# Output projection regrouped into passes of six and two heads, a later square sum for retention heads, one Newton square on ScalarE, and the norm weights stored behind x's first rows

## The chip, the core and the metric

The kernel runs on one core of a Trainium2 chip. The core has a matrix engine (PE), a vector engine (DVE), a scalar engine (ACT), a general engine (POOL) and a queue engine (SP) that issues most transfers. Each engine works through its own program in order and waits on semaphores for the others. The metric is device time in microseconds (us) of one execution; lower is better. Times before: 1225.84 us, the median of three runs (1225.83 to 1226.55). Matrix products are accumulated in PSUM, of which there are eight banks of 128 x 512 float32.

## What is computed

Two layers over 512 tokens of width 1024, float32. Cut to what matters here:

```python
for l in range(DEPTH):
    h = rms_norm(x, norm1_g[l])
    rq, rk, rv, rg, sq, sk, sv = jnp.split(h @ w_in[l], IN_SPLITS, axis=-1)
    ret = chunk_retention(rotary(rq), rotary(rk), rv)          # 4 heads of 128
    ret = head_group_norm(ret, ret_norm_g[l]) * jax.nn.silu(rg)
    sb = head_rms_norm(stick_breaking(sq, sk, sv), sb_norm_g[l])  # 4 heads of 128
    x = x + jnp.concatenate([ret, sb], axis=-1) @ w_out[l]
    h = rms_norm(x, norm2_g[l])
    x = x + (jax.nn.silu(h @ w_gate[l]) * (h @ w_up[l])) @ w_down[l]
return rms_norm(x, final_g)
```

## The kernel before

All activations lie transposed, features on the 128 partitions and the 512 tokens along the row: `x` is eight tiles of 128 x 512, one for each 128 features. Every float32 matrix is split into a high and a low part (`hi` rounded by ACT, `lo = src - hi` by DVE or POOL), and one product of 128 x 128 by 128 x 512 is three matrix instructions (`mm3`, L188). The weights come as 205 units of 128 x 1024 (`WeightStream`, L98): SP loads a unit into `wraw`, ACT rounds it into `whi` (L130), DVE takes `wlo` (L131). There are three `whi`/`wlo` buffers, so the conversion of a unit can start when PE is through with the unit three before it. 24 matrix instructions use up one unit.

PE's order is written out by hand. `Stream` (L149) counts the planned time of what has been emitted, and `pe.later(delay, fn)` puts a piece of work into the stream once that much planned time has passed. The orders of the other engines are made by a scheduler at build time and are fixed in the program.

In the attention half of a layer PE computes, head by head, the projections of four stick-breaking heads (keys 4 to 7 of `mix`) and then of four retention heads (keys 0 to 3). A retention head h goes through these steps:

- `rotated` (L430): its q and its k come off the `acc` banks by DVE (L433 to L435, results `t1` and `t2`), POOL adds the two (L437), ACT rounds the sum (`qhi`, `khi`, L288), POOL takes the rest (`qlo`, `klo`, L289).
- `retain` (L561), D_RQK = 9000 ns after its k: PE forms the scores in `z` banks (the *score products*), DVE multiplies them with the decay (`p`, four instructions, L578), ACT and DVE split them (`pthi`, `ptlo`).
- `mixed` (L583), D_RAV = 9000 ns later: PE multiplies the scores with v into the bank `o`, 12 instructions. They are called the *weighted products* W0 to W3 below, for heads 0 to 3. DVE reads `o` into `m` (L587), and `normed` (L480) has ACT square `o` (L483), ACT and POOL split the square (`shi`, `slo`).
- `finish` (L488), D_SS = 5500 ns later: PE sums the squares over the features with two products by ones, again into the bank `o`. They are called the *square sum* SS0 to SS3. Then ACT takes Ln and Exp (L313, L314), and DVE refines the result by one Newton step (L315, L318, L321) and multiplies `m` (L494); ACT and DVE split `m` into `mix[h]`.

There is one bank with the tag `o`. W0, SS0, W1, SS1, W2, SS2, W3, SS3 follow each other in it: SS h can be written when L587 and L483 have read W h, and W h+1 can be written when Ln (L313) and the Newton instruction that reads the sum (L318) are done with SS h.

The output projection (L628 to L642) makes 8 x 8 products. First a pass over all eight output tiles d with the four stick-breaking heads, added to `x` (L632). Then, in two groups of four tiles, a pass with retention heads 0 to 2 for each tile, a drain of what is still due in the stream, and the products of head 3, added to `x` (L641); `feed` (L297) then prepares the tile for the FFN. The products of the first pass lie among the steps of the last retention heads and cover their chains.

At the start ACT issues the transfer of the norm weights `gcol` (128 x 48, L242), SP those of `x` and the first weight units. PE runs 12 warm-up products (`WARM`) without use. The first conversions follow in the order `hhi[0]` from x and `gcol` (L291), a square for the norm (L301), `whi` of the first unit in two halves.

Of the kernel before, what the change touches and what calls it, by code (L numbers as in the profile page):

```python
# [38 lines left out]
BY_KEY = ((0,), (1, 3), (2,))  # L39
WARM = 12  # L40
RAW = 4
D_SQK, D_TURN, D_STEP, D_SAV = 5000, 11500, 2000, 5000
D_RQK, D_RAV, D_SS = 9000, 9000, 5500

# [4 lines left out]
def block_plan():  # L49
# [6 lines left out]
    for l in range(L):  # L56
# [5 lines left out]
        for h in range(NH):  # L62
            plan += cols("w_in", l, RQ + h * HD) + cols("w_in", l, RK + h * HD)
        for d in range(KT):
            plan += [("w_out", l, NH + k, d * P, P) for k in range(NH)]
        for d0 in range(0, KT, 4):
            ds = range(d0, d0 + 4)
            plan += [("w_out", l, k, d * P, P) for d in ds for k in range(NH - 1)]
            plan += [("w_out", l, NH - 1, d * P, P) for d in ds]
        for k in range(KT):  # L70
# [27 lines left out]
class WeightStream:  # L98
# [11 lines left out]

    def load(self, upto, step=UW):
        for i in range(len(self.raw), min(upto, len(self.units))):
            w = sum(b[4] for b in self.units[i])
            raw = self.rawpool.tile([P, UW], F32, tag="wraw", name=f"wraw{i}", bufs=RAW)
            for a in range(0, w, step):
                c = slice(a, min(a + step, w))
                load = self.nc.sync.dma_start(out=raw[:, c], in_=self.ws[i, :, c])
            self.raw.append((raw, w))
            self.loads.append(load.ins)

    def split(self, upto, step=UW):
        nc = self.nc
        self.load(upto)
        for i in range(len(self.ready), min(upto, len(self.units))):
            raw, w = self.raw[i]
            hi = self.pool.tile([P, UW], F32R, tag="whi", name=f"whi{i}", bufs=3)
            lo = self.pool.tile([P, UW], F32R, tag="wlo", name=f"wlo{i}", bufs=3)
            for a in range(0, w, step):
                c = slice(a, min(a + step, w))
                copy = nc.scalar.copy(out=hi[:, c], in_=raw[:, c])  # L130
                nc.vector.tensor_tensor(  # L131
                    out=lo[:, c], in0=raw[:, c], in1=hi[:, c].bitcast(F32), op=ALU.subtract
                )
# [15 lines left out]
class Stream:  # L149
# [20 lines left out]
    def run(self, i):  # L170
        self.inside = True
        self.tasks.pop(i)[1]()
        self.inside = False

    def drain(self):
        while self.tasks:
            self.run(min(range(len(self.tasks)), key=lambda n: self.tasks[n][0]))

# [26 lines left out]
@with_exitstack  # L205
def layers(ctx, tc, xT_in, ws_in, gcol_in, gfin_in, cos_in, sin_in, dec_in, out):
    nc = tc.nc
# [32 lines left out]

    gcol = const.tile([P, L * NG], F32, name="gcol")
    nc.scalar.dma_start(out=gcol, in_=gcol_in)  # L242
    table_set(EXP_LN)
    idle = const.tile([P, S], BF16, name="idle")
    nc.vector.memset(idle, 0.0)
    x = [keep.tile([P, S], F32, name=f"x{k}", tag=f"x{k}") for k in range(KT)]
    for k in range(KT):
        nc.sync.dma_start(out=x[k], in_=xT_in[:, k, :])
        if k == 0:
            wst.load(1, step=512)  # L250
        elif k % 2 == 0:
            wst.load(1 + k // 2)
# [29 lines left out]
    def banks_b():  # L282
        return [bank() for _ in range(3)] + [bank("o", 1)]
# [60 lines left out]
    def attention(l):  # L344
        g0 = l * NG
        with tc.tile_pool(name=f"at{l}", bufs=1, reuse_waits="tile") as sb:
# [4 lines left out]
            def temp(name, bufs=4):  # L351
                return sb.tile([P, S], F32, tag="tmp", name=name, bufs=bufs)
# [127 lines left out]
            def normed(o, m, key):  # L480
# [147 lines left out]
            for d in range(KT):  # L628
# [4 lines left out]
            for d0 in range(0, KT, 4):  # L633
# [188 lines left out]
```

## Time and profile before

| | |
|---|---|
| runs, median | 1225.84 us |
| the profiled execution | 1226.61 us |
| its span, first to last instruction | 1224.8 us |
| PE busy | 1210.2 us, 99% of the span |
| DVE busy | 692.4 us, 57% |
| ACT busy | 489.4 us, 40% |
| POOL busy | 154.0 us, 13% |
| chain that ended last | PE 94%, DVE 4%, ACT 1%, DMA 1% |

The profile is read here in four steps. The page tells which engine fills the span. The list of waits of PE tells what it waits for. The timelines of the engines around such a wait tell which instruction in which queue was late. The view of stretches gives the granted PE clock, at 1.00 for 2.4 GHz and at 0.50 for 1.2 GHz. The profile models the end of a product 0.16 us after the next one can start, so a wait that it lists is about that much shorter than what PE loses. Layer 1 repeats layer 0 about 602.9 us later.

### The profile page before, as it was taken

What the parts mean: (1) busy time and instruction counts of PE and PEld (TensorE: products, weight loads), DVE (VectorE), ACT (ScalarE), POOL (GpSimd) and SP (SyncE); (2) the same over time, 40 slices, a digit from 0 to 9 for tenths busy, and PEclk for the clock granted to TensorE, in tenths of its full rate; (3) what the DMA queues carried; (4) which work ended last, traced back from release to release, by engine and by line L of the source; (5) the groups of instructions that cost most, each with busy time, mean ns of one, the idle gap of its engine ahead of it and who ended that gap; (6) DMA issues with size and microseconds to landing.
All of it is one profiled execution on the core that took longest, in us unless ns stands there. A gap on an engine that the chain in (4) does not pass through costs nothing.

```text
span 1224.8 us, 13905 instructions
## 1 busy us (share of the span) xinstructions
PE 1210.2 (99%) x5476; PEld 998.5 (82%) x5476; DVE 692.4 (57%) x868; ACT 489.4 (40%) x708; POOL 154.0 (13%) x135
## 2 busy tenths in 40 slices
PE   9999999999999999999999999999999999999997
PEld 6888887888888888888888888878888888888886
DVE  6566899774443344444444778997644433444433
ACT  6467644453331222323335755445432312223323
POOL 1122054120000000000121212523100000000021
PEclk9999999999999999999999999999999999999999
DMA  7321221223222222233232122213222223332311
GB/s 258 104 69 69 87 87 69 69 103 104 88 102 102 88 103 93 97 104 107 100 109 80 70 80 75 86 69 103 104 86 89 101 80 105 108 102 88 103 69 69
DMA packets 33329, 115.74 MB, mean 94 GB/s; under 512 B 3824, under 2 KB 3824, under 8 KB 33264
## 3 DMA queue, kind: packets, MB, share of 16 engines
q1 hardware_dynamic: 33120, 114.83, 27.1%
q8 instruction: 43, 0.70, 0.2%
q14 instruction: 22, 0.18, 0.0%
q10 hardware_dynamic: 144, 0.02, 0.0%
HBM read 112.75 MB, written 2.10 MB: 94 GB/s over the span
## 4 chain that ended last, share of the span: by engine, by line
PE 94%; DVE 4%; issue 1%; ACT 1%; DMA 1%; POOL 0%; SPq 0%; DVEq 0%; ACTq 0%
PE acc L185 73%; PE z L185 16%; PE o L185 5%; PE z L196 1%; DMA wraw<-ws 1%; DVE ptlo L289 1%; DVE wlo L131 1%; DVE u L315 0%; DVE mlo L289 0%; POOL slo L289 0%; DVE m L587 0%; DVE t L435 0%; DVE t L433 0%; DVE p L578 0%; DVE rn L321 0%
## 5 line engine op out<-in xcount | busy, mean ns | idle before, releaser
L130 ACT CAST whi<-wraw 128x1024 fp32r<-128x1024 f32 (+1 forms) x205 | 214.7, 1048 | 495.7 <-PE acc L185 225.1
L185 PE MATMUL acc<-hhi,whi 128*128 128x512 f32 x960 | 376.0, 392 | 0.0
L185 PE MATMUL acc<-hhi,wlo 128*128 128x512 f32 x960 | 373.9, 389 | 0.0
L185 PE MATMUL acc<-hlo,whi 128*128 128x512 f32 x960 | 373.8, 389 | 0.0
L131 DVE TENSOR_TENSOR wlo<-wraw,whi 128x1024 fp32r<-128x1024 f32 (+1 forms) x205 | 256.9, 1254 | 132.8 <-ACT whi L130 132.0
L185 PEld LDWEIGHTS acc<-hhi,wlo 128*128 128x128 f32 x960 | 180.2, 188 | 38.0
L185 PEld LDWEIGHTS acc<-hhi,whi 128*128 128x128 f32 x960 | 180.4, 188 | 36.3
L185 PEld LDWEIGHTS acc<-hlo,whi 128*128 128x128 f32 x960 | 180.4, 188 | 36.0
L691 DVE TENSOR_TENSOR u<-acc,rs 128x512 f32<-128x512 f32 x40 | 27.7, 692 | 134.4 <-PE acc L185 134.4
L305 POOL TENSOR_TENSOR ssq<-ssq,sqx 128x512 f32<-128x512 f32 x21 | 33.9, 1613 | 383.3 <-ACT sqx L304 382.8
L688 DVE TENSOR_TENSOR g<-acc,rs 128x512 f32<-128x512 f32 x40 | 27.7, 692 | 89.8 <-PE acc L185 89.8
L185 PE MATMUL acc<-ahi,whi 128*128 128x512 f32 x176 | 68.5, 389 | 0.0
L185 PE MATMUL acc<-alo,whi 128*128 128x512 f32 x176 | 68.5, 389 | 0.0
L185 PE MATMUL acc<-ahi,wlo 128*128 128x512 f32 x176 | 68.5, 389 | 0.0
L755 POOL TENSOR_TENSOR xtd<-xtd,gfin 128x512 f32<-128x512 f32 x7 | 10.2, 1453 | 345.7 <-ACT fsq L751 345.7
L292 DVE SCALAR_TENSOR_TENSOR hlo<-x,gcol,hhi 128x512 fp32r<-128x512 f32 x32 | 34.9, 1099 | 8.2 <-ACT hhi L291 8.2
L185 PEld LDWEIGHTS acc<-ahi,wlo 128*128 128x128 f32 x176 | 33.0, 188 | 6.9
L185 PEld LDWEIGHTS acc<-ahi,whi 128*128 128x128 f32 x176 | 33.0, 188 | 6.8
L185 PEld LDWEIGHTS acc<-alo,whi 128*128 128x128 f32 x176 | 33.0, 188 | 6.8
L288 ACT CAST ahi<-u 128x512 fp32r<-128x512 f32 x44 | 27.4, 622 | 28.1 <-DVE u L692 28.1
L185 PE MATMUL acc<-mhi,whi 128*128 128x512 f32 x88 | 35.8, 406 | 0.0
L185 PE MATMUL acc<-mhi,wlo 128*128 128x512 f32 x88 | 35.6, 405 | 0.0
(190 smaller groups left out, 1817.1 us busy)
## 6 DMA issues: line engine op xcount, KB each, us to landing
wraw<-ws SPq DMA_DIRECT2D x203, 512.0 KB, 3.5
x<-xT SPq DMA_DIRECT2D x8, 256.0 KB, 7.0
dec<-dec SPq DMA_DIRECT2D x8, 256.0 KB, 3.6
out<-ob SPq DMA_DIRECT2D x4, 512.0 KB, 2.6
wraw<-ws SPq DMA_DIRECT2D x2, 256.0 KB, 4.1
cosrs<-cos SPq DMA_DIRECT2D x2, 256.0 KB, 4.7
sinrs<-sin SPq DMA_DIRECT2D x2, 256.0 KB, 4.9
gfin<-gfin SPq DMA_DIRECT2D x1, 512.0 KB, 4.4
```

Of the source, the lines that this page charges most:

```text
L130: copy = nc.scalar.copy(out=hi[:, c], in_=raw[:, c])
L131: nc.vector.tensor_tensor(out=lo[:, c], in0=raw[:, c], in1=hi[:, c].bitcast(F32), op=ALU.subtract)
L185: self.nc.tensor.matmul(ps, lhsT=lhsT, rhs=rhs, start=start, stop=stop)
L196: self.nc.tensor.transpose(out, src, ident)
L288: nc.scalar.copy(out=hi, in_=src)
L289: eng.tensor_tensor(out=lo, in0=src, in1=hi.bitcast(F32), op=ALU.subtract)
L292: eng.scalar_tensor_tensor(out=lo, in0=src, scalar=scale, in1=hi.bitcast(F32), op0=ALU.mult, op1=ALU.subtract,)
L305: eng.tensor_tensor(out=ssq, in0=ssq, in1=q, op=ALU.add)
L688: nc.vector.tensor_tensor(out=g, in0=pg, in1=rs, op=ALU.mult)
L691: nc.vector.tensor_tensor(out=u, in0=pu, in1=rs, op=ALU.mult)
L755: nc.gpsimd.tensor_tensor(out=y, in0=y, in1=gfin[:, c], op=ALU.mult)
```

## The change

1. **Passes.** The eight output tiles are no longer gone through with the four stick-breaking heads first. A pass of six heads (`FIRST`: 4 to 7 and 0, `NEXT`: 1) goes over all tiles; in its first three tiles head 1 is held back until the other fifteen products are out. A pass of two heads (2 and 3) follows: over tiles 0 to 3 head 2, a drain, head 3; over tiles 4 to 7 both at once. The order of the weights in memory follows. The number of products and of additions to `x` is the same.
2. **Square sum later.** For retention heads the delay of `finish` is 9000 ns (`D_RSS`) in place of 5500.
3. **Newton.** In `normed` the first instruction of the Newton step (`-0.5/n * r * r`, L315 on DVE) becomes a Square on ACT, and the last two (L321, L494) are folded so that three DVE instructions are left of four. The results lie in two of the four `tmp` buffers.
4. **Start.** The norm weights lie behind the first 128 rows of x in one tile `xg` of 128 x 560, one transfer. x's second tile is issued between the two halves of the first weight unit. The first square is placed behind the rounding of the first half. `WARM` is 10.

```diff
-D_RQK, D_RAV, D_SS = 9000, 9000, 5500
+D_RQK, D_RAV, D_SS, D_RSS = 9000, 9000, 5500, 9000
+FIRST, NEXT = tuple(range(NH, 2 * NH)) + (0,), (1,)
+OUT = [((0, 1, 2), FIRST), ((0, 1, 2), NEXT), (range(3, KT), FIRST + NEXT)]
+OUT += [(range(4), (2,)), (range(4), (3,)), (range(4, KT), (2, 3))]
...
+            with tc.issue_after(wst.first_copy) if g == 0 else nullcontext():
+                nc.scalar.activation(out=ssq, in_=x[k], func=AF.Square)
...
-                    rn = temp("rn")
-                    rsqrt(rn, ss, HD)
-                    nc.vector.tensor_tensor(out=m, in0=m, in1=rn, op=ALU.mult)
+                    r, t = temp("rn"), temp("sq")
+                    nc.scalar.activation(out=r, in_=ss, func=AF.Ln, scale=1.0 / HD, bias=eps)
+                    nc.scalar.activation(out=r, in_=r, func=AF.Exp, scale=-0.5)
+                    nc.scalar.activation(out=t, in_=r, func=AF.Square, scale=0.125)
+                    nc.vector.scalar_tensor_tensor(
+                        out=t, in0=ss, scalar=HD * EPS, in1=t, op0=ALU.add, op1=ALU.mult
+                    )
+                    nc.vector.scalar_tensor_tensor(
+                        out=t, in0=t, scalar=6.0, in1=r, op0=ALU.subtract, op1=ALU.mult
+                    )
+                    nc.vector.scalar_tensor_tensor(
+                        out=m, in0=m, scalar=-0.25, in1=t, op0=ALU.mult, op1=ALU.mult
+                    )
...
-                pe.later(D_SS, finish)
+                pe.later(D_RSS if key < NH else D_SS, finish)
...
+                while k not in mix:
+                    pe.advance()
...
+    def advance(self):
+        self.run(min(range(len(self.tasks)), key=lambda n: self.tasks[n][0]))
...
+    xg = keep.tile([P, S + L * NG], F32, name="xg", tag="xg")
+    gcol = xg[:, S:]
...
+            wst.load(1, step=512, x1=lambda: nc.sync.dma_start(out=x[1], in_=xT_in[:, 0, :]))
...
+            def add(d, ps):
+                nc.vector.tensor_tensor(out=x[d], in0=x[d], in1=ps, op=ALU.add)
...
-            for d in range(KT):
-                ps = bank()
-                for k in range(NH):
-                    out_step(ps, d, NH + k, k == 0, k == NH - 1)
-                nc.vector.tensor_tensor(out=x[d], in0=x[d], in1=ps, op=ALU.add)
-            for d0 in range(0, KT, 4):
-                pss = dict(zip(range(d0, d0 + 4), banks_b() if d0 else banks_a()))
-                for d, ps in pss.items():
-                    for k in range(NH - 1):
-                        out_step(ps, d, k, k == 0, False)
-                pe.drain()
-                for d, ps in pss.items():
-                    out_step(ps, d, NH - 1, False, True)
-                    nc.vector.tensor_tensor(out=x[d], in0=x[d], in1=ps, op=ALU.add)
-                    feed(d, g0 + 8)
+            half = FIRST + NEXT
+            pss = [bank() for _ in range(3)]
+            for d, ps in enumerate(pss):
+                for k in FIRST:
+                    out_step(ps, d, k, k == half[0], False)
+            for d, ps in enumerate(pss):
+                for k in NEXT:
+                    out_step(ps, d, k, False, k == half[-1])
+                add(d, ps)
+            for d in range(3, KT):
+                ps = bank()
+                for k in half:
+                    out_step(ps, d, k, k == half[0], k == half[-1])
+                add(d, ps)
+            pss = banks_a()
+            for d, ps in enumerate(pss):
+                out_step(ps, d, 2, True, False)
+            pe.drain()
+            for d, ps in enumerate(pss):
+                out_step(ps, d, 3, False, True)
+                add(d, ps)
+                feed(d, g0 + 8)
+            for d in range(4, KT):
+                ps = bank()
+                out_step(ps, d, 2, True, False)
+                out_step(ps, d, 3, False, True)
+                add(d, ps)
+                feed(d, g0 + 8)
```

How this moves instructions is shown at two places of layer 0, as the built programs have them. Line numbers of the changed program are its own there: L193 is `mm` (L185 before), L133 and L135 are the rounding of a weight unit and its rest, L301 and L302 a split, L447 to L449 `rotated`, L497 the square of `o`, L507 to L516 the new `finish`, L611 is L587, L655 is `add`.

PE, place one, SS0 and what follows it in the program before (`acc` products are the projections of the last retention heads):

```order
L185 MATMUL acc<-hhi_130,wlo_1598 128x512
L185 MATMUL o<-shi,ones_r 128x512
L185 MATMUL o<-slo,ones_r 128x512
L185 MATMUL acc<-hhi_131,whi_1597 128x512
L185 MATMUL acc<-hlo_139,whi_1597 128x512
L185 MATMUL acc<-hhi_131,wlo_1598 128x512
```

The same place now, as far as the first product of W1:

```order
L193 MATMUL acc<-hhi_134,wlo_1590 128x512
L193 MATMUL o<-shi,ones_r 128x512
L193 MATMUL o<-slo,ones_r 128x512
L193 MATMUL acc<-hhi_127,whi_1631 128x512
L193 MATMUL acc<-hlo_135,whi_1631 128x512
L193 MATMUL acc<-hhi_127,wlo_1632 128x512
L193 MATMUL acc<-hhi_128,whi_1631 128x512
L193 MATMUL acc<-hlo_136,whi_1631 128x512
L193 MATMUL acc<-hhi_128,wlo_1632 128x512
L193 MATMUL o<-pthi,vhi 128x512
```

Before, 24 products lie between SS0 and W1 and 18 between the score products and SS0; now 6 lie between SS0 and W1 and 36 ahead of SS0. In the same way the products between SS1 and W2 go from 27 to 9, and those between SS2 and W3 from 33 to 12.

ACT, place one, from the rounding of a weight unit ahead of SS0's Ln (`r<-o`) to the square of W1, before:

```order
L130 CAST whi_1736<-wraw_1643 128x1024
L313 ACTIVATE r<-o,eps 128x512
L314 ACTIVATE r<-r 128x512
L288 CAST khi<-k 128x512
L130 CAST whi_1794<-wraw_1740 128x1024
L288 CAST mhi<-m 128x512
L483 ACTIVATE sq<-o 128x512
```

The same now (`rn<-o` is the Ln, `sq<-rn` the new Square):

```order
L133 CAST whi_1728<-wraw_1635 128x1024
L301 CAST khi<-k 128x512
L133 CAST whi_1785<-wraw_1732 128x1024
L507 ACTIVATE rn<-o,eps 128x512
L508 ACTIVATE rn<-rn 128x512
L509 ACTIVATE sq<-rn 128x512
L301 CAST mhi<-m 128x512
L497 ACTIVATE sq<-o 128x512
```

The rounding of head 2's k and of a weight unit, which stood behind Ln and Exp, stand ahead of them now.

ACT, place two, around SS1's Ln, before:

```order
L288 CAST pthi<-p 128x256
L130 CAST whi_1907<-wraw_1798 128x1024
L313 ACTIVATE r<-o,eps 128x512
L314 ACTIVATE r<-r 128x512
L130 CAST whi_1941<-wraw_1911 128x1024
L288 CAST mhi<-m 128x512
L288 CAST khi<-k 128x512
```

The same now:

```order
L301 CAST qhi<-q 128x512
L133 CAST whi_1884<-wraw_1789 128x1024
L301 CAST khi<-k 128x512
L507 ACTIVATE rn<-o,eps 128x512
L508 ACTIVATE rn<-rn 128x512
L133 CAST whi_1929<-wraw_1888 128x1024
L509 ACTIVATE sq<-rn 128x512
L301 CAST mhi<-m 128x512
```

Head 3's k, which was rounded behind SS1's chain, is rounded ahead of it now, and a weight unit lies between Exp and Square.

DVE, place two, from the split scores of head 2 to what releases the bank `o` after SS1, before (L318 releases it):

```order
L289 TENSOR_TENSOR ptlo<-p,pthi 128x512 x2
L289 TENSOR_TENSOR ptlo<-p,pthi 128x256
L131 TENSOR_TENSOR wlo_1908<-wraw_1798,whi_1907 128x1024
L315 SCALAR_TENSOR_TENSOR u<-r 128x512
L318 SCALAR_TENSOR_TENSOR u<-o,u 128x512
```

The same now (`sq<-o,sq` releases it):

```order
L302 TENSOR_TENSOR ptlo<-p,pthi 128x512 x2
L302 TENSOR_TENSOR ptlo<-p,pthi 128x256
L447 TENSOR_TENSOR t_1870<-acc,cosrs 128x512
L448 TENSOR_TENSOR t_1871<-acc,sinrs 64x512
L449 TENSOR_TENSOR t_1871<-acc,sinrs 64x512
L135 TENSOR_TENSOR wlo_1885<-wraw_1789,whi_1884 128x1024
L135 TENSOR_TENSOR wlo_1930<-wraw_1888,whi_1929 128x1024
L510 SCALAR_TENSOR_TENSOR sq<-o,sq 128x512
```

The rotation of head 3's k and two weight units stand ahead of the releasing instruction now, where one weight unit and L315 stood. At place one, ahead of SS0's `sq<-o,sq`, two weight units and one rotation (L447, of head 3's q) stand behind head 2's rotated k; before it was one unit and L315. Ahead of SS2's `sq<-o,sq` stand four additions to `x`, the fourth of them of tile 3.

## Rows read from the trace of the kernel before

**Rows 1.** The page, part 1: busy time, share of the span, instructions.

```profile
PE 1210.2 (99%) x5476; PEld 998.5 (82%) x5476; DVE 692.4 (57%) x868; ACT 489.4 (40%) x708; POOL 154.0 (13%) x135
```

**Rows 2.** PE's waits over the span: total us, times, longest.

```profile
PE o L185 <- ACT shi L288: 2.6, 2, 1.3
PE o L185 <- POOL slo L289: 2.1, 2, 1.1
...
PE o L185 <- DVE u L318: 0.8, 2, 0.4
PE z L185 <- DVE wlo L131: 0.2, 1, 0.2
```

**Rows 3.** PE's timeline: start, us, instruction, in brackets the idle time before.

```profile
173.09 0.39 PE L185 MATMUL o<-pthi,vhi 128*128 128x512 f32 x1
...
176.79 0.40 PE L185 MATMUL acc<-hhi,whi 128*128 128x512 f32 x1
...
187.39 0.50 PE L185 MATMUL o<-pthi,vhi 128*128 128x512 f32 x1 [0.41 <-DVE u L318]
...
196.80 0.50 PE L185 MATMUL o<-shi,ones_r 128*128 128x512 f32 x1 [1.31 <-ACT shi L288]
198.35 0.80 PE L185 MATMUL o<-slo,ones_r 128*128 128x512 f32 x1 [1.05 <-POOL slo L289]
```

**Rows 4.** Stretches behind that wait, both layers; granted clock behind POOL's column.

```profile
197.90:201.20 3.30, 2.85 (x7) 2.27 (x8) 3.30 (x3) 2.46 (x4) 2.09 (x2) 0.50 0.00 0
...
802.10:805.40 3.30, 3.30 (x10) 2.52 (x8) 3.27 (x4) 1.02 (x2) 0.74 (x1) 0.50 0.08 17
```

**Rows 5.** Chain that ended last: start, us, engine; one row of undisturbed products.

```profile
240.17 6.12 PE acc L185 x27
```

**Rows 6.** ACT's timeline around SS0.

```profile
176.05 0.60 ACT L483 ACTIVATE sq<-o 128x512 f32<-128x512 f32 x1 [4.66 <-DVE m L587]
...
181.57 0.69 ACT L313 ACTIVATE r<-o,eps 128x512 f32<-128x512 f32 x1 [1.00 <-PE o L185]
182.29 0.63 ACT L314 ACTIVATE r<-r 128x512 f32<-128x512 f32 x1
186.09 0.62 ACT L288 CAST khi<-k 128x512 fp32r<-128x512 f32 x1 [3.18 <-POOL k L437]
186.62 1.04 ACT L130 CAST whi<-wraw 128x1024 fp32r<-128x1024 f32 x1
```

**Rows 7.** POOL's timeline, same place.

```profile
183.74 2.32 POOL L437 TENSOR_TENSOR k<-t,t 128x512 f32<-128x512 f32 x1 [2.37 <-DVE t L435]
186.79 1.28 POOL L289 TENSOR_TENSOR klo<-k,khi 128x512 fp32r<-128x512 f32 x1 [0.73 <-ACT khi L288]
```

**Rows 8.** DVE's timeline, same place, and one later row.

```profile
175.26 0.75 DVE L587 SCALAR_TENSOR_TENSOR m<-o,gcol,gate 128x512 f32<-128x512 f32 x1 [1.28 <-PE o L185]
175.93 1.78 DVE L578 TENSOR_TENSOR p<-z,dec 128x512 f32<-128x512 f32 x4
177.63 4.02 DVE L289 TENSOR_TENSOR ptlo<-p,pthi 128x512 fp32r<-128x512 f32 x3
181.58 0.68 DVE L433 TENSOR_TENSOR t<-acc,cosrs 128x512 f32<-128x512 f32 x1
...
183.69 1.23 DVE L131 TENSOR_TENSOR wlo<-wraw,whi 128x1024 fp32r<-128x1024 f32 x1
184.83 1.78 DVE L315 SCALAR_TENSOR_TENSOR u<-r 128x512 f32<-128x512 f32 x1
186.64 0.69 DVE L318 SCALAR_TENSOR_TENSOR u<-o,u 128x512 f32<-128x512 f32 x1
...
213.73 2.04 DVE L289 TENSOR_TENSOR ptlo<-p,pthi 128x512 fp32r<-128x512 f32 x3
```

**Rows 9.** Chain that ended last, in its first 20 us.

```profile
3.07 7.12 DMA wraw<-ws
...
19.91 4.16 PE z L185 x17
```

More of the change, by code (lines that the diff above doesn't have):

```diff
@@ L63, in block_plan @@
             plan += cols("w_in", l, RQ + h * HD) + cols("w_in", l, RK + h * HD)
-        for d in range(KT):
-            plan += [("w_out", l, NH + k, d * P, P) for k in range(NH)]
-        for d0 in range(0, KT, 4):
-            ds = range(d0, d0 + 4)
-            plan += [("w_out", l, k, d * P, P) for d in ds for k in range(NH - 1)]
-            plan += [("w_out", l, NH - 1, d * P, P) for d in ds]
+        for ds, ks in OUT:
+            plan += [("w_out", l, k, d * P, P) for d in ds for k in ks]
         for k in range(KT):
@@ L117, in load @@
                 load = self.nc.sync.dma_start(out=raw[:, c], in_=self.ws[i, :, c])
+                if x1 and a == 0:
+                    x1()
             self.raw.append((raw, w))
@@ L130, in split @@
                 copy = nc.scalar.copy(out=hi[:, c], in_=raw[:, c])
+                first = copy.ins if a == 0 else first
                 nc.vector.tensor_tensor(
@@ L135, in split @@
             self.copies.append(copy.ins)
+            self.first_copy = first
     def block(self, *key):
@@ L173, in run @@
         self.inside = False
+    def advance(self):
+        self.run(min(range(len(self.tasks)), key=lambda n: self.tasks[n][0]))
     def drain(self):
         while self.tasks:
-            self.run(min(range(len(self.tasks)), key=lambda n: self.tasks[n][0]))
+            self.advance()
     @staticmethod
@@ L205, in layers @@
 @with_exitstack
-def layers(ctx, tc, xT_in, ws_in, gcol_in, gfin_in, cos_in, sin_in, dec_in, out):
+def layers(ctx, tc, xg_in, xT_in, ws_in, gfin_in, cos_in, sin_in, dec_in, out):
     nc = tc.nc
@@ L239, in layers @@
     EXP_LN, SILU = "natural_log_exp_and_others", "silu_and_others"
-    gcol = const.tile([P, L * NG], F32, name="gcol")
-    nc.scalar.dma_start(out=gcol, in_=gcol_in)
     table_set(EXP_LN)
@@ L245, in layers @@
     nc.vector.memset(idle, 0.0)
-    x = [keep.tile([P, S], F32, name=f"x{k}", tag=f"x{k}") for k in range(KT)]
+    xg = keep.tile([P, S + L * NG], F32, name="xg", tag="xg")
+    gcol = xg[:, S:]
+    x = [keep.tile([P, S], F32, name=f"x{k}", tag=f"x{k}") for k in range(1, KT)]
+    x.insert(0, xg[:, :S])
     for k in range(KT):
-        nc.sync.dma_start(out=x[k], in_=xT_in[:, k, :])
         if k == 0:
-            wst.load(1, step=512)
-        elif k % 2 == 0:
+            nc.sync.dma_start(out=xg, in_=xg_in)
+            continue
+        if k == 1:
+            wst.load(1, step=512, x1=lambda: nc.sync.dma_start(out=x[1], in_=xT_in[:, 0, :]))
+        else:
+            nc.sync.dma_start(out=x[k], in_=xT_in[:, k - 1, :])
+        if k > 1 and k % 2 == 0:
             wst.load(1 + k // 2)
@@ L300, in feed @@
         if k == 0:
-            nc.scalar.activation(out=ssq, in_=x[k], func=AF.Square)
+            with tc.issue_after(wst.first_copy) if g == 0 else nullcontext():
+                nc.scalar.activation(out=ssq, in_=x[k], func=AF.Square)
         else:
@@ L810 @@
     cos, sin, dec = shape_constants()
-    arrays = {"xT": x, "ws": ws, "gcol": gcol, "gfin": gfin, "cos": cos, "sin": sin, "dec": dec}
+    xg = np.ascontiguousarray(np.concatenate([x[:, 0], gcol], axis=1))
+    x = np.ascontiguousarray(x[:, 1:])
+    arrays = {"xg": xg, "xT": x, "ws": ws, "gfin": gfin, "cos": cos, "sin": sin, "dec": dec}
     nc = bacc.Bacc("TRN2", target_bir_lowering=False, num_devices=1, dynamic_dma_scratch_size=1024)
```

6 lines of the change are left out of this document (2 added, 4 removed).

## The prediction

> **What bounds the kernel now.** The page comes first: PE is busy for 99% of the span [rows 1], and the number of products does not change. Undisturbed, 27 products of 512 columns take 6.12 us, 0.227 each [rows 5]. A change of order can therefore win or lose only what PE waits, and the clock. PE's waits, read next, are few: in each layer 1.3 us for `shi`, 1.05 for `slo` and 0.4 for L318 [rows 2]. PE's timeline puts them: 187.39 is W1, which waits for the bank `o`; 196.80 and 198.35 are SS1, which comes before its square is ready [rows 3]. Each of the three costs some 0.16 more than listed (product 0.39 long, next one after 0.227). Behind SS1 the granted clock is 0.50, in both layers [rows 4]; a stretch of 3.3 us at half pace costs half, 1.5 to 1.6. Sum per layer: 2.75 + 0.5 + 1.5 = **4.8 us**, 9.5 in all. That is the most the passes can win. Last I read the queues of ACT, DVE and POOL around SS0 [rows 6 to 8], since they decide when the bank is free.
>
> **The passes and the later square sum.** Removed: SS1's wait. SS1 was due at 196.80 - 1.31 - 0.16 = 195.3 and had its two operands 1.5 and 2.8 us later [rows 3]; now 18 more products, 4.1 us, stand ahead of it. Gain 2.35 + 0.3 + 1.5 of clock a layer. But the same move pulls each square sum up to the next weighted product, and both need the one bank. From the second product of SS0 to W1 the least chain is: 0.46 to Ln's start (before: 176.79 + 19 x 0.227 = 181.1 to 181.57), 0.72 Ln, 0.65 Exp, 0.60 Square, 0.69 for the releasing DVE instruction, 0.06 [rows 6, 8]: 3.2 us. PE has 0.23 + 6 x 0.227 = 1.6 us of work there; before it had 24 products, 5.7. So W1 waits at least **1.6**; W2 (9 products, 2.3 us) at least **0.9**; W3 (12) at least **0.3**. These are the lower ends.
>
> The queues make it longer. *W1.* W0 at 173.09, projections from 176.79 [rows 3], now 36 of them: SS0 at 184.96, W1 due at 184.96 + 0.45 + 1.36 = **186.8**. Up to there all queues stand as before. Head 2's k leaves POOL at 186.06; ACT rounds it at 186.09 and a weight unit from 186.62 to 187.66 [rows 6, 7]. Both stand ahead of Ln in the changed program: Ln 187.6, Exp 188.3, Square 189.0 to 189.6. DVE has the rest of that unit first, from 187.7, which shares POOL's time with `klo` (186.79 to 188.07) [rows 7], 1.23 long [rows 8], to 189.2, then a rotation, 0.68, to 189.9. The releasing instruction ends at 190.3 (by ACT) to 190.6 (by DVE). W1 starts near 190.5: a wait of **3.7**, bounds 1.6 and 4.0. I take the queue's value, because the rows that hold Ln back are the trace's own.
>
> *W2.* From W1's start, PE's own work to W2 is W1 and scores 3.70 (173.09 to 176.79 [rows 3]), 3 + 15 + 18 + 9 products 10.2, SS1 0.45: 14.4. The other engines need: W1 1.9 and 0.3 to the first read, but DVE is still in head 0's three Newton instructions, two rotations and `mlo`, six of 0.7 from 189.9, so `m` ends at 194.9; `p` and three `ptlo` 5.65 (175.93 to 181.58), where POOL works beside them, against some 3.7 where three `ptlo` take 2.04 in place of 4.02 [rows 8]; the rotation of head 3's k, 2.1 (181.58 to 183.69); k on POOL beside a weight unit, 2.4 from the unit's start (183.69 to 186.06); its rounding, Ln, Exp, a weight unit, Square, 0.6 + 0.7 + 0.65 + 0.95 + 0.6 = 3.5; DVE's rest of that unit 0.7 past the Square's end; the release 0.7. That is 194.9 + 5.65 + 2.1 + 2.4 + 3.5 + 1.4 = 209.9, against 190.5 + 14.4 = 204.9. I take the crowded 5.65, since `slo` and head 3's q fall on POOL in the same microseconds, as at 177.63. Wait **5.0**, bounds 0.9 and 5.5; with 3.7 it is 3.0.
>
> The Trainium skill, page "SBUF — State Buffer", section "Who interferes with whom", states that a DVE instruction with two SBUF inputs and a GpSimd instruction that reads SBUF block each other for a whole instruction. The 4.02 against 2.04 of [rows 8] agrees. By it W2 waits 5.0, and 3.0 if the two do not meet.
>
> *W3.* Ahead of the release DVE has the addition of tile 3, whose products end 9 after SS2, 2.0 us; add 0.35 to the read, 0.69, 0.69: 3.7 from SS2's end, and PE has 12 products, 2.7. Wait **1.0**, bounds 0.3 and 1.5. Head 3's result still has 39 products of cover behind SS3, but its rounding now waits behind a weight unit that PE frees 27 products after SS3 (6.1 us, then 1.04 + 1.23 + 0.6 + 0.7 in ACT and DVE, against the 9.1 at which `mlo` is read): **0.25**, bounds 0 and 1.
>
> *Clock.* The waits of SS1 brought it to 0.50 [rows 4]; the 0.4 at W1 did not. Idle stretches of 3.7 and 5.0 are longer than either, so I expect a fall behind W1 and one behind W2, 1.5 each, bounds 0 and 3.4 together. The first is mostly hidden: PE slower behind W1 only shortens W2's wait. I count one, **1.5**.
>
> Sum per layer: 3.7 + 5.0 + 1.0 + 0.25 + 1.5 = 11.4, less 4.8 = **+6.6**; two layers +13.2.
>
> **The rest.** *Newton:* sixteen norms, one DVE instruction less each (0.69, or 1.78 where POOL works beside it [rows 8]) and one ACT instruction of 0.60 more. ACT is busy 40%, DVE 57% [rows 1]; in the chain above Square takes L315's place, so it gains nothing by itself. Around the stick-breaking heads PE has no wait: the four of [rows 2], with that for the first product, are all it lists, and 24 products or more lie behind each square sum: cost 0, and up to 0.5 a layer if that cover is thinner than it looks. *Passes at the end:* x is added at the same count; tiles 4 to 7 come every 6 products (1.36 us) while DVE needs some 1.75 for an addition, a split and its quarter of a unit, at 0.69, 0.75 and 1.23 for instructions of such shapes [rows 8]. The lag of 1.6 us is covered by the FFN's first 12 products for each k, 2.7 us: 0. *Start:* `hhi` waits no longer for `gcol`, and a Square of 0.60 [rows 6] no longer lies ahead of the first weights: the first product comes some 0.6 us earlier. But PE stops for `wlo` at 19.91, on a chain that begins with the landing of the second unit at 10.19 [rows 9], the sixth transfer in SP's queue before and after. What is won early is waited there: -0.2 of the stop of 0.2 + 0.16 seen now [rows 2], bounds -0.5 and +0.5. Two warm-up products less: 0 behind the same stop, up to +1.5 if the clock rises later.
>
> **Sum.** The profiled execution took 1226.61 for a span of 1224.8, 1.8 outside it, and lies 0.8 above the median of the runs, 1225.84. 13.2 - 0.2 = +13.0 gives 1239.6 for it and **1239** for the median.
>
> **Rivals.**
> *Faster.* The intended one: k reaches ACT early enough that Ln starts with SS0, so each weighted product waits only for the least chain. For: W1's 187.39 shows PE released 0.06 behind the DVE instruction. Against: khi at 186.09 is a row, and its place ahead of Ln is in the program. Price per layer 1.6 + 0.9 + 0.3 = 2.8 without a fall of the clock, against 4.8: 1225.84 - 4.0 - 0.2 = **1221.6**. It decides where the three waits and the clock stay under 4.8 a layer, which needs Ln at SS0's end or shortly behind it.
>
> The Trainium skill, page "TensorE: Matmul & The Clock Gate", section "Architectural detail: the array is 16× 32×32, not 1× 128×128", calls the queues of ACT and DVE strict first-in first-out. That speaks against this rival; by it Ln stays behind the weight unit.
>
> *Slower by less.* POOL and DVE hardly meet behind W1. W1 3.5, W2 2.0 to 3.0, partly the first fall of the clock, W3 0.3 to 1.0, one fall that counts: 6.5 to 8.3 a layer, +1.7 to +3.5: **1229 to 1233**.
> *No change.* The waits add up to what they replace, 4.8 a layer: **1225 to 1227**. It needs W2 at its lower end and one fall.
> *Slower by more.* Both falls count and the end of the passes slips: 14 to 15 a layer, **1244 to 1246**.
>
> **How the numbers follow.** Forecast (1234 to 1243) 0.57, slower by less 0.18, slower by more 0.06, no change 0.08, faster 0.11. About 0.2%, 2.5 us, is what a measurement of this kernel can tell from no change. Faster 0.11, same 0.08, slower 0.81. The range from 1229 to 1246 leaves out the faster case and no change, 0.19 together, and holds the unknown costs of W2 and the clock.
>
> **What would show it.** In the list of PE's waits: no wait for `shi` or `slo`, but two long ones for the new DVE instruction that reads `o` in each layer, near 3.5 and 4.8, and a shorter third. In ACT's timeline Ln of SS0 behind khi and a weight unit, 2 us after its sum is ready. Two falls of the clock in each layer. Wrong, if Ln of SS0 starts within 0.5 us of the sum, if W2 waits less than 2 us, or if a wait of PE appears among the stick-breaking heads or at the start that none of this has.

## The result and the profile after

| | before | after |
|---|---|---|
| runs, median (lowest to highest) | 1225.95 us (1225.83 to 1226.55) | 1243.32 us (1240.04 to 1244.11) |
| the profiled execution | 1226.61 us | 1243.66 us |
| its span | 1224.8 us | 1241.9 us |
| mean granted PE clock | 0.996 | 0.990 |

The changed kernel is slower: 1.0134 times the time before, 95% interval 1.0119 to 1.0149, so 17 us. The forecast was 1239, the range 1229 to 1246. Direction, place and mechanism came out as forecast; the terms for the end of the passes, the clock and the start did not.

PE's waits of the kernel after (total us, times, longest) answer to [rows 2]:

```profile
PE o L193 <- DVE sq L510: 13.8, 6, 3.4
PE o L193 <- DVE sslo L302: 3.5, 2, 1.8
PE o L350 <- DVE idle L251: 1.2, 1, 1.2
PE z L193 <- DVE wlo L135: 0.6, 2, 0.3
```

The waits for `shi` and `slo` are gone. In their place stand three waits a layer for L510, the new DVE instruction that releases the bank `o`, and one a layer for `sslo`, the low part of the FFN's sum of squares, which was not in the forecast. PE's timeline, layer 0 (start, us, instruction, idle time before), has W1, W2, W3 and the second product of the FFN's square sum:

```profile
189.47 0.80 PE L193 MATMUL o<-pthi,vhi 128*128 128x512 f32 x1 [3.41 <-DVE sq L510]
...
209.87 0.80 PE L193 MATMUL o<-pthi,vhi 128*128 128x512 f32 x1 [2.92 <-DVE sq L510]
...
228.74 0.50 PE L193 MATMUL o<-pthi,vhi 128*128 128x512 f32 x1 [0.68 <-DVE sq L510]
...
271.25 0.50 PE L193 MATMUL o<-sslo,ones_r 128*128 128x512 f32 x1 [1.77 <-DVE sslo L302]
```

Counted from start to start, less the pace of 0.227 [rows 5], the losses are 3.58, 3.09, 0.85 and 1.95 us; in layer 1 3.59, 2.81, 0.85 and 1.92. ACT's timeline around SS0 answers to [rows 6]:

```profile
185.17 0.62 ACT L301 CAST khi<-k 128x512 fp32r<-128x512 f32 x1 [5.55 <-POOL k L451]
185.70 1.04 ACT L133 CAST whi<-wraw 128x1024 fp32r<-128x1024 f32 x1
186.65 0.68 ACT L507 ACTIVATE rn<-o,eps 128x512 f32<-128x512 f32 x1
187.36 0.63 ACT L508 ACTIVATE rn<-rn 128x512 f32<-128x512 f32 x1
188.02 0.63 ACT L509 ACTIVATE sq<-rn 128x512 f32<-128x512 f32 x1
```

DVE's timeline at the same place answers to [rows 8]:

```profile
186.77 1.45 DVE L135 TENSOR_TENSOR wlo<-wraw,whi 128x1024 fp32r<-128x1024 f32 x1 [2.79 <-ACT whi L133]
188.14 0.68 DVE L447 TENSOR_TENSOR t<-acc,cosrs 128x512 f32<-128x512 f32 x1
188.74 0.67 DVE L510 SCALAR_TENSOR_TENSOR sq<-o,sq 128x512 f32<-128x512 f32 x1
```

The queue is the one that the prediction wrote down: `khi`, a weight unit, and only then Ln; on DVE the rest of the unit and a rotation ahead of the release. Its times come 0.93 us earlier, since the start of the kernel won that much. The stretches behind W1 in layer 0, and behind W1 in layer 1, answer to [rows 4] (the granted clock stands behind POOL's column):

```profile
188.50:191.80 3.30, 2.33 (x6) 2.04 (x7) 3.19 (x6) 0.77 (x2) 0.00 (x0) 0.50 0.48 159
191.90:195.20 3.30, 3.30 (x12) 2.91 (x11) 1.83 (x3) 0.92 (x2) 0.00 (x0) 0.50 0.00 0
...
802.90:806.20 3.30, 3.30 (x12) 3.02 (x12) 3.19 (x5) 0.62 (x1) 0.00 (x0) 0.50 0.37 146
```

At 0.50 products of 512 columns start 0.43 us apart (193.16, 193.59 and 194.01 in PE's timeline), where 0.227 is their pace at full clock. In layer 0 the clock stays at 0.50 for 6.8 us behind W1 and for 6.8 behind W2, in layer 1 for 3.4 behind each; before it was 3.4 once a layer. The five runs, 1240 to 1244 us, have mean clocks of 0.994 to 0.990.

### The profile page after: what moved, and what is told of

Same layout as the page of the kernel before. It is cut to its first block, busy times and chain, and to the rows that moved or that the text cites. A ratio compares the mean times of both kernels' runs of the same rounds, so it can differ in the third digit from the quotient of the medians.

```text
span 1241.9 us, 13918 instructions
## 1 busy us (share of the span) xinstructions
PE 1215.2 (98%) x5474; PEld 1002.6 (81%) x5474; DVE 667.6 (54%) x852; ACT 499.1 (40%) x724; POOL 150.8 (12%) x135
## 4 chain that ended last, share of the span: by engine, by line
PE 90%; DVE 4%; POOL 2%; issue 1%; ACT 1%; DMA 0%; SPq 0%; ACTq 0%; POOLq 0%; DVEq 0%
PE acc L193 71%; PE z L193 13%; PE o L193 5%; DVE wlo L135 1%; DVE hlo L305 1%; PE z L204 1%; POOL k L451 1%; DVE x L655 1%; POOL qlo L302 1%; POOL slo L302 0%; DMA x<-xT 0%; POOL q L451 0%; ACT whi L133 0%; DVE sq L510 0%; DVE p L602 0%
## 5 line engine op out<-in xcount | busy, mean ns | idle before, releaser
L133 ACT CAST whi<-wraw 128x1024 fp32r<-128x1024 f32 (+1 forms) x205 | 214.2, 1045 | 471.9 <-PE acc L193 223.3
L193 PE MATMUL acc<-hhi,whi 128*128 128x512 f32 x960 | 376.2, 392 | 0.0
L193 PE MATMUL acc<-hhi,wlo 128*128 128x512 f32 x960 | 374.3, 390 | 0.0
L193 PE MATMUL acc<-hlo,whi 128*128 128x512 f32 x960 | 374.0, 390 | 0.0
L135 DVE TENSOR_TENSOR wlo<-wraw,whi 128x1024 fp32r<-128x1024 f32 (+1 forms) x205 | 258.0, 1259 | 151.3 <-ACT whi L133 150.6
L193 PEld LDWEIGHTS acc<-hhi,wlo 128*128 128x128 f32 x960 | 180.4, 188 | 38.0
L193 PEld LDWEIGHTS acc<-hhi,whi 128*128 128x128 f32 x960 | 180.6, 188 | 36.4
L193 PEld LDWEIGHTS acc<-hlo,whi 128*128 128x128 f32 x960 | 180.5, 188 | 36.1
L193 PE MATMUL acc<-ahi,whi 128*128 128x512 f32 x176 | 68.5, 389 | 0.0
L193 PE MATMUL acc<-alo,whi 128*128 128x512 f32 x176 | 68.5, 389 | 0.0
L193 PE MATMUL acc<-ahi,wlo 128*128 128x512 f32 x176 | 68.5, 389 | 0.0
L193 PE MATMUL acc<-mhi,whi 128*128 128x512 f32 x112 | 45.0, 402 | 0.0
L193 PE MATMUL acc<-mlo,whi 128*128 128x512 f32 x112 | 44.8, 400 | 0.0
L193 PE MATMUL acc<-mhi,wlo 128*128 128x512 f32 x112 | 44.7, 399 | 0.0
L301 ACT CAST ahi<-u 128x512 fp32r<-128x512 f32 x44 | 27.3, 621 | 28.4 <-DVE u L734 28.4
L193 PEld LDWEIGHTS acc<-ahi,wlo 128*128 128x128 f32 x176 | 33.0, 188 | 6.9
L193 PEld LDWEIGHTS acc<-ahi,whi 128*128 128x128 f32 x176 | 33.0, 188 | 6.8
L193 PEld LDWEIGHTS acc<-alo,whi 128*128 128x128 f32 x176 | 33.0, 188 | 6.8
```

What stands on the lines that cost most here:

```text
L135: nc.vector.tensor_tensor(out=lo[:, c], in0=raw[:, c], in1=hi[:, c].bitcast(F32), op=ALU.subtract)
L193: self.nc.tensor.matmul(ps, lhsT=lhsT, rhs=rhs, start=start, stop=stop)
L301: nc.scalar.copy(out=hi, in_=src)
```

## Experiments

Theory T: the square sum that comes later meets the weighted product in the one bank `o`, and each weighted product waits for the queues of ACT and DVE to release it. The rivals laid the loss to the passes or the new Newton step. Each time below is a median with its range; ratios are to runs of the kernel before beside it, whose medians are 1226.35 to 1226.67 us.

**1. The delay taken back.**

```diff
-D_RQK, D_RAV, D_SS, D_RSS = 9000, 9000, 5500, 9000
+D_RQK, D_RAV, D_SS, D_RSS = 9000, 9000, 5500, 5500
```

> The changed kernel with the square sum of the retention heads back at 5500 ns; passes, Newton step and start stay changed. Theory (late square sum and one bank o): the waits of W1 to W3 for the DVE instruction that reads o fall from 3.4, 2.9 and 0.7 us to 0.5 or less, SS1's waits for shi and slo come back with one fall of the clock per layer, as before; the wait of the FFN's square sum (1.8 a layer) and the 0.9 won at the start stay: 1225.95 - 0.9 + 3.9 = 1229, from 1227 to 1231. Rival passes: the new grouping of the output projection makes the waits by itself, they stay over 2 us and the time over 1237. Rival Newton: Square on ACT and the two tmp buffers make them, the same over 1237.

Measured 1228.58 us (1227.09 to 1230.35), ratio 1.002 (1.001 to 1.003). PE's waits of this run:

```profile
PE o L193 <- DVE sslo L302: 3.6, 2, 1.8
PE o L193 <- DVE sq L510: 2.2, 2, 1.1
PE o L193 <- POOL slo L302: 2.1, 2, 1.1
PE o L193 <- ACT shi L301: 1.3, 2, 0.6
```

One number undone gives back 14.7 of the 17.4 us. The wait for `sslo` stays: it is not the delay's. Of the waits of W1 to W3 one of 1.1 us a layer is left, at W1, where the expectation had 0.5 or less; the new Newton step alone makes the same one (run 8).

**2. The delay alone**, in the kernel before.

```diff
-D_RQK, D_RAV, D_SS = 9000, 9000, 5500
+D_RQK, D_RAV, D_SS, D_RSS = 9000, 9000, 5500, 9000
...
-                pe.later(D_SS, finish)
+                pe.later(D_RSS if key < NH else D_SS, finish)
```

> The kernel before with one change: the square sum of the retention heads at 9000 ns. Theory: W1 and W2 wait 2.5 to 4.5 us each for the Newton instruction that reads o, W3 up to 1, with two falls of the clock per layer, SS1 no longer waits: +5 to +8 a layer, 1236 to 1242. Rival passes and rival Newton: nothing of theirs is in it, so the waits stay as before and the time within 1224 to 1227.

Measured 1251.58 us (1249.8 to 1253.75), ratio 1.0209 (1.0192 to 1.0226): 9.6 us more than the top of T's range. PE's waits of this run:

```profile
PE o L185 <- DVE u L318: 16.2, 6, 3.8
PE z L185 <- ACT mhi L288: 6.0, 2, 3.0
```

The first line is T's, on the old releasing instruction L318. The second is what T lacked: in the old passes only 15 products, 3.4 us, stand between head 3's square sum and the first product that reads its result, so the last head's own late sum stalls PE 3.15 us a layer, and 0.5 more for `mlo`: 7.3 us in both layers. The passes of six and two hide that: after has no such line. It is what they are good for beside the late sum; alone they save nothing (run 7).

**3. A bank of its own** for the retention square sums.

```diff
-                    ss = bank("o", 1)
+                    ss = bank("z", 4) if key < NH else bank("o", 1)
```

> The changed kernel with the square sums of the retention heads in one of the four z banks, so that the weighted products no longer share a bank with them. Theory: no wait at W1, W2 and W3, no wait at SS1, no fall of the clock there; the wait of the FFN's square sum stays: 1225.95 - 9.6 - 0.9 + 3.9 = 1219.4, from 1217 to 1222. Rival passes or Newton: PE waits for mix, the scores or the additions in place of the bank, over 1230.

Measured 1223.15 us (1222.62 to 1225.25), ratio 0.9977 (0.9966 to 0.9988): 20 us back, and 0.2% faster than before. Ln of SS0 still starts 1.9 us behind the end of its sum, but no wait of PE ends at it. PE's waits of this run that are left beside the warm-up's:

```profile
PE o L193 <- DVE sslo L302: 3.5, 2, 1.8
PE o L193 <- DVE ptlo L302: 1.7, 2, 0.8
```

`sslo` is not the bank's and stays. The time lies above the expected range of 1217 to 1222. The 3.7 us above the sum of 1219.4 are for the most part the second line: with the bank free W2 comes early, and its products with the last split scores (202.94 in PE's timeline) wait for `ptlo`, 1.04 us a layer; products some 7 us later lose another 0.7 in steps of 0.1 to 0.2. The clock of this run is 0.999, without a fall in either layer.

**4. The FFN's square sum twelve products later.**

```diff
-                if k == 3:
+                if k == 4:
```

> The changed kernel with the FFN's square sum over the features behind its fifth k (12 products, 2.7 us, later) and nothing else. Theory (the two-head pass leaves DVE and POOL 24 products less cover between the first addition of tile 0 and this sum): the wait of 1.8 us for sslo in each layer is gone, the others stay: 1243.3 - 3.9 = 1239.4, from 1237 to 1241. Rival (the chain behind the sum is late as well, and the FFN's first gate waits in its place): no gain, 1242 to 1245.

Measured 1238.92 us (1238.27 to 1241.9), ratio 1.0107 (1.0091 to 1.0122); 4.4 less than after, against 3.9 expected; the runs of both spread over about 4 us, so the 0.5 between the two can't be told. The wait for `sslo` is gone from the list; PE's timeline shows the two products next to each other:

```profile
270.89 0.40 PE L193 MATMUL o<-sshi,ones_r 128*128 128x512 f32 x1
271.13 0.39 PE L193 MATMUL o<-sslo,ones_r 128*128 128x512 f32 x1
```

**5. The start alone**, in the kernel before (part 4 of the change, as in its diff).

> The kernel before with all the edits to its start and nothing else (norm weights in the transfer of x's first rows, the two halves of the first weight unit around x's second rows, the first square behind the first rounding, ten warm-up products). Theory S: the whole of the 0.93 us by which W0 starts earlier in the kernel after comes from these edits and nothing behind them takes it back: 1225.4 us beside 1226.35 for the kernel before (1225.1 to 1225.8), the second unit's rounding at about 9.2 us and not 10.2. Rival: what the start gains is lost at the first wait in layer 0 that hangs on POOL or DVE and not on TensorE: 1226.3 (1226.1 to 1226.6).

Measured 1225.25 us (1224.81 to 1225.59), ratio 0.9988 (0.9980 to 0.9997): 1.3 won, inside T's range. ACT's timeline has the second unit's rounding at 8.41. Not all of the 1.3 need be the start's: in this run's trace layer 1 has no stretch at 0.50, and a new wait of 0.7 us for `klo` instead.

**6. Only the norm weights moved into x's first transfer**, in the kernel before.

```diff
-    gcol = const.tile([P, L * NG], F32, name="gcol")
-    nc.scalar.dma_start(out=gcol, in_=gcol_in)
...
+        nc.sync.dma_start(out=x[k] if k else xg, in_=xT_in[:, k - 1, :] if k else xg_in)
```

> The kernel before with the norm weights in the transfer of x's first rows alone; the order of the transfers, the place of the first square and the twelve warm-up products stay. Theory A: the separate transfer of the norm weights from ScalarE's queue is what held the others back by 1 us, so the second unit is rounded from about 9.2 us, and the time is that of the run with all start edits, 1225.4 us (1225.0 to 1225.8). Theory B: the order of the transfers does it, and this edit alone gives 1226.35 (1226.1 to 1226.6) with the second unit at 10.2 us.

Measured 1225.36 us (1224.96 to 1225.63), ratio 0.9989 (0.9980 to 0.9997): the whole gain of run 5. DMA issues of the first 6 us (KB each, median us to landing), before:

```profile
q10 hardware_dynamic: 144, 0.02, 4.2%
...
wraw<-ws SPq DMA_DIRECT2D x2, 512.0 KB, 7.4
...
gcol<-gcol ACTq DMA_DIRECT2D x1, 24.0 KB, 4.0
```

The same view of this run:

```profile
wraw<-ws SPq DMA_DIRECT2D x2, 512.0 KB, 5.7
...
xg<-xg SPq DMA_DIRECT2D x1, 280.0 KB, 2.8
```

ACT's timeline of this run, where it rounds the second unit:

```profile
8.37 1.03 ACT L130 CAST whi<-wraw 128x1024 fp32r<-128x1024 f32 x1
```

A transfer of 24 KB in 144 packets from a second queue is gone, and weight units of 512 KB land in 5.7 and not 7.4 us; the second unit is rounded from 8.37 and not 10.21. The traces of the other runs bear it out: in the four kernels with the separate transfer (before, 2, 7, 8) the second unit lands at 9.85 to 10.55 us, in the nine without it (after, 1, 3 to 6, 9 to 11) at 8.20 to 8.98. Theory A holds.

**7. The passes alone**, in the kernel before (part 1, with the order of the weights).

> The kernel before with the output projection in passes of six and two heads alone: square sums as early as before, Newton steps and start as before. Theory T: the passes bring the new wait of the FFN's square sum, 1.9 us a layer, since the first sum x + projection comes 81 and not 105 products ahead of it, and move nothing else: 1226.35 + 3.9 = 1230.2 us (1229 to 1231.5). Rival: that wait comes from the later retention square sums or the new Newton step, and the passes alone leave the time as it is: 1226.4 (1225.5 to 1227.2).

Measured 1230.17 us (1228.42 to 1232.52), ratio 1.0028 (1.0019 to 1.0037). PE's list gains one line of weight over [rows 2]:

```profile
PE o L189 <- DVE sslo L293: 3.6, 2, 1.8
```

So the passes alone cost 3.6 us here, at the FFN, and save nothing.

**8. The new Newton step alone**, in the kernel before (part 3).

> The kernel before with the new Newton step alone (Square on ScalarE, three VectorE instructions in place of four). Theory T: no wait of TensorE ends at these instructions while the square sums come early, so nothing moves: 1226.35 us (1225.9 to 1226.9). Rival: the Square on ScalarE puts 0.63 us ahead of the release of the bank, and that reaches the weighted product behind each of the first three retention square sums, up to 0.6 us in each: 1229 us (1227.5 to 1230).

Measured 1225.65 us (1224.86 to 1226.31), ratio 0.9993 (0.9984 to 1.0002): no difference that can be told. Its list shows a trade; W1 waits longer and the sum behind it less:

```profile
PE o L185 <- DVE sq L496: 2.3, 2, 1.1
PE o L185 <- POOL slo L289: 2.1, 2, 1.0
PE o L185 <- ACT shi L288: 1.3, 2, 0.6
```

W1 starts 0.7 us later, `shi` is waited for 0.7 less. The rival's mechanism is there, 0.7 us at W1, but costs nothing.

**9. Ln ahead of the weight unit**, in the kernel after (`behind` issues the rounding after the named instruction).

```diff
-                copy = nc.scalar.copy(out=hi[:, c], in_=raw[:, c])
+                with self.behind(self.guard) if self.guard else nullcontext():
+                    copy = nc.scalar.copy(out=hi[:, c], in_=raw[:, c])
+                self.guard = None
...
+                    if key < NH:
+                        wst.guard = square.ins
```

> The kernel after with the rounding of a weight unit that stands between the retention square sum and its Ln on ScalarE put behind that square sum's Ln, Exp and Square (the rounding of k stays ahead). Theory T: the bank is released late because ScalarE works in order, and the weight unit's 0.95 us is part of W1's and W2's wait: W1 waits 2.6 and not 3.6 us, W2 about 2.1 and not 3.0, so 1243.3 - 3.8 = 1239.5 us (1237 to 1241.5). Rival: Ln starts late for another reason (the second square-sum product waits for its low part from POOL), the order on ScalarE changes nothing, or the weight unit that is now late stops TensorE for as long: 1243 us (1241.5 to 1245).

Measured 1234.7 us (1233.73 to 1236.14), ratio 1.0066 (1.0052 to 1.0080). ACT's timeline of this run, around SS0:

```profile
184.87 0.62 ACT L305 CAST khi<-k 128x512 fp32r<-128x512 f32 x1 [5.56 <-POOL k L455]
185.39 0.68 ACT L511 ACTIVATE rn<-o,eps 128x512 f32<-128x512 f32 x1
186.10 0.63 ACT L512 ACTIVATE rn<-rn 128x512 f32<-128x512 f32 x1
186.76 0.63 ACT L513 ACTIVATE sq<-rn 128x512 f32<-128x512 f32 x1
187.30 1.03 ACT L135 CAST whi<-wraw 128x1024 fp32r<-128x1024 f32 x1
```

PE's timeline of this run, W1:

```profile
188.17 0.80 PE L196 MATMUL o<-pthi,vhi 128*128 128x512 f32 x1 [2.42 <-DVE sq L516]
```

W1 waits 2.60 in both layers, as T said. W2 waits 1.77 and 2.83, where T had 2.1 in both: in layer 1 it is no shorter than after. The waits alone give back 3.3 us. The gain of 8.6, and 7.5 between the two spans, is larger because the clock falls less: this run has 0.50 for 6.8 us behind W1 in layer 0 and for 3.4 behind W2 in layer 1, half of the 20.5 us of the run after. Half of the 10.2 us that are gone is 5.1, less what PE would have idled in them: an estimate of 4 to 4.5.

**10. Both repairs**, runs 3 and 4 together.

> The kernel after with both repairs, the square sums of the retention heads in a score bank of their own and the FFN's square sum one group of twelve products later. Theory T: the two losses are at different places and add up, so the second repair takes its 3.9 us here too: 1223.15 - 3.9 = 1219.3 us (1218.3 to 1220.5). Rival: with the bank's waits gone the FFN's square sum comes earlier against the x additions, and one group of twelve products doesn't cover it: 1221.5 (1220.5 to 1223).

Measured 1219.17 us (1218.87 to 1219.28), ratio 0.9940 (0.9928 to 0.9952). The two losses are separate and add up.

**11. The old passes with a bank of its own** for all four square sums, the longer delay for heads 0 to 2 alone, Newton step and start as after. Two places, against the kernel before:

```diff
-                pe.later(D_SS, finish)
+                pe.later(D_RSS if key < NH - 1 else D_SS, finish)
...
-                    ss = bank("o", 1)
+                    ss = bank("z", 4) if key < NH else bank("o", 1)
```

> The kernel before, its passes of the output projection kept (four stick-breaking heads, then three retention heads, then the last), with the edits to the start, the new Newton step, the later square sums for the first three retention heads alone, and these in a score bank of their own. Theory T: what the later square sums are good for is the cover for their low part, and only the bank stood against it; the passes of six and two are needed only where the last head's square sum is late too. So the waits of 0.57, 1.47 and 1.33 us and the clock's 1.5 us behind them go in each layer, the start gives 1.1, and the wait for ptlo of 1.0 us a layer comes as in the run with a bank of its own: 1226.4 - 9.7 - 1.1 + 2.1 = 1217.7 us (1215.5 to 1220). Rival: in the old passes the products of the third head are due before its later square sum is finished, some 3 us a layer: 1223 us (1221 to 1225).

Measured 1217.4 us (1217.07 to 1219.54), ratio 0.9930 (0.9917 to 0.9942): the fastest of all, 0.7% under the kernel before, 2.1% under the kernel after. What is left in PE's list of waits beside the warm-up's:

```profile
PE o L189 <- DVE ptlo L298: 1.6, 2, 0.8
PE z L189 <- DVE wlo L134: 0.2, 1, 0.2
```

No wait for a square sum is left at all, and the clock does not fall in either layer. The intention behind the later square sum was right; it needed a bank and no new passes. Some 1.3 of the 9.3 us are the start's (run 5). A bank of its own without the later sum was not run.

## Why the prediction was right, and where it was wrong

| term | predicted | measured |
|---|---|---|
| Ln of SS0; W1, in the time of before | 187.6; 190.5 | 186.65 + 0.93 = 187.6; 189.47 + 0.93 = 190.4 |
| W1, a layer | 3.7 | 3.58, 3.59 |
| W2, a layer | 5.0, or less by what the first fall of the clock hides | 3.09, 2.81 |
| from W1 to W2 | 14.4 + 5.0 = 19.4 | 20.40, 19.02 |
| W3, a layer | 1.0 | 0.85, 0.85 |
| head 3's result, a layer | 0.25 | no wait seen |
| clock, a layer | one fall counted, 1.5 | 13.7 us at 0.50 in layer 0, 6.8 in layer 1; half of it, less PE's idle time, is some 5.8 and 3.4 |
| passes at the end, a layer | 0 | **1.95, 1.92** |
| start | -0.2, bounds -0.5 and +0.5 | **-0.93** |

*The attention part* was right in its mechanism. From W0 to the first product of the FFN's square sum, the same number of products in both kernels, it is 88.7 us before and 96.9 after in layer 0 (173.09 to 261.78, 172.16 to 269.07), and 88.9 and 94.5 in layer 1: +8.2 and +5.6, together +13.8, where +13.2 was forecast. That the sum comes so close is in part luck: +6.6 was forecast for each layer, and one came out above it and one below, as the clock fell for 13.7 us in the one and 6.8 in the other. Runs 1 and 2 show that the delay makes it, run 3 that the shared bank does, and run 9 that the place of Ln behind a weight unit on ACT is 1.0 us of W1. The page of the Trainium skill "TensorE: Matmul & The Clock Gate", section "Architectural detail: the array is 16× 32×32, not 1× 128×128", by whose strict first-in first-out queues Ln stays behind the unit, agrees with the timelines of after (Ln 1.9 us behind the end of its sum) and of run 9 (1.0).

*W2* was forecast as 5.0 of which the slow clock would hide a part. The trace has it so: from W1 to W2 it is 20.4 and 19.0, against 14.4 of PE's own work, and the slow products behind W1 fill the 2.9 and 1.8 that are not waits.

*The clock* was mis-sized. One fall of 1.5 was counted a layer; layer 0 has 13.7 us at half clock in this run and layer 1 6.8. The spread of the five runs, 4.1 us against 0.7 before, goes with it: the longer the run, the lower its mean clock. What made layer 0's stretches twice as long is not settled: the waits ahead of them are of nearly the same length in both layers (3.58 and 3.59, 3.09 and 2.81).

*The passes at the end* are the step that failed, in two ways. First, "the lag of 1.6 us is covered by the FFN's first 12 products for each k" looked only at what each group of the FFN's products reads. It left out the square sum behind the first 48 of them, which needs all eight tiles, and each addition on the way. The new second pass puts 81 products (18.4 us) between its first addition to `x` and that sum, the old passes 105 (23.8 us). DVE's timeline before has the last addition 0.6 us behind its products (250.66 + 0.39 in PE's timeline), and `sslo` there ahead of its own product, by 261.78 + 0.23 - 260.85 = 1.2 us:

```profile
251.68 0.68 DVE L641 TENSOR_TENSOR x<-x,o 128x512 f32<-128x512 f32 x1
...
260.17 0.68 DVE L289 TENSOR_TENSOR sslo<-ssq,sshi 128x512 fp32r<-128x512 f32 x1
```

Second, the lag itself is 4.7 us and not 1.6. After, the last products of tile 7 end at 257.97 + 0.39 in PE's timeline, and DVE adds them from 263.07:

```profile
263.07 0.67 DVE L655 TENSOR_TENSOR x<-x,acc 128x512 f32<-128x512 f32 x1
263.66 1.19 DVE L305 SCALAR_TENSOR_TENSOR hlo<-x,xg,hhi 128x512 fp32r<-128x512 f32 x1
264.77 2.32 DVE L135 TENSOR_TENSOR wlo<-wraw,whi 128x1024 fp32r<-128x1024 f32 x1
267.02 2.44 DVE L305 SCALAR_TENSOR_TENSOR hlo<-x,xg,hhi 128x512 fp32r<-128x512 f32 x2
269.38 1.21 DVE L135 TENSOR_TENSOR wlo<-wraw,whi 128x1024 fp32r<-128x1024 f32 x1
270.51 0.68 DVE L302 TENSOR_TENSOR sslo<-ssq,sshi 128x512 fp32r<-128x512 f32 x1
```

DVE has no pause between 250.9 and the end of `sslo`, 1.9 us behind the place of its product. The prediction took 0.75 for a split of `x` and 1.23 for a weight unit; POOL adds up squares at the same time, and here most splits take 1.2 to 1.8 and two units 2.2 and 2.3. The kernel before has such lengths too, and two weight units behind its last addition as well, but its additions come in two groups of four, 48 products apart, and DVE has caught up when the second begins (it waits 0.19 us for PE at 249.05).

Run 7 shows that the passes alone bring this wait, run 4 that twelve products of cover take it away. Taking it in would have given 1239 + 3.9 - 0.7 = 1242 us.

*The start* was mis-sized. The prediction held the landing of the second unit at 10.19 for fixed, as the sixth transfer in SP's queue. It came a microsecond earlier: ACT's timeline after has x's first rows at 3.59 (before 4.75) and the second unit at 9.17. The 4.75 was the norm weights' own doing: x's rows had landed at 4.54 and they at 4.72, so they held the first conversion back too.

```profile
3.59 0.72 ACT L304 ACTIVATE hhi<-xg 128x512 fp32r<-128x512 f32 x1 [1.57 <-DMA xg<-xg]
...
9.17 1.03 ACT L133 CAST whi<-wraw 128x1024 fp32r<-128x1024 f32 x1
```

Run 6 lays this to the transfer of the norm weights and to nothing else in the start.

*Newton* was right: cost 0 (run 8).

*The rivals.* The faster one needed Ln of SS0 at the sum's end; with the later sum it starts 1.9 us behind it in each trace, and 1.0 in run 9. The one named "slower by more", both falls counting and the end of the passes slipping, had a chance of 0.06 and is what happened in kind: each layer has two falls, and the end slips by 1.9. At 1244 to 1246 it was priced just above the median. So the time stood inside the range, but above the 1234 to 1243 that the forecast itself held.

The sum closes: +13.8 + 3.9 - 0.9 = +16.8 of the 17.1 us between the two spans.

## What to carry to other kernels

Moving a step later in order to cover its input lost here until its output had a buffer of its own (runs 2, 3 and 11): look for who else needs the bank, and read the releasing instruction's place in its engine's queue, since that queue set the wait here. When a pass is cut so that results come closer to the end, check the one consumer that needs all of them, not the first that needs some, and price the engine that delivers them with the lengths its instructions have when its neighbours are busy. A tiny transfer on a second queue beside the start's large ones can cost more than what it carries; give it a ride with another.

## What was not expected of the hardware

One transfer of 24 KB in 144 packets, issued from ACT's queue at 0.73 us, went with longer landings of the 512 KB units issued beside it (median 7.2 to 7.9 us in the four traces that have it, 5.7 to 6.4 in the nine that do not), and cost 1.2 us of the kernel's time (run 6). The page of the Trainium skill "DMA: Bandwidth & Descriptors", section "Rules for kernel authors", says that small transfers should be joined into large ones, being mostly overhead; runs 5 and 6 agree in that joining it was faster, by 1.3 and 1.2 us; what they show is a loss of the other queue's transfers, not what the small one costs by itself. How it comes about was not tried.

The clock at 0.50 does not follow from the wait alone: with the same waits of 1.3 and 1.05 us in both layers [rows 2], the kernel before has a stretch at 0.50 in both, the run with the new start (5) in layer 0 only and the run with one transfer (6) in layer 1 only. In these two a new wait of 0.7 us for `klo` stands in the layer without the fall, which takes back part of what the missing stretch is worth.
